# A planner that orders a four-layer transformer block: exclusive PSUM banks, gathered modulation matmuls, settled operands, sixteen passes

## The chip, the core and the metric

The kernel runs on one core of one Trainium2 chip. The time is device microseconds for one execution. Five instruction queues matter: TensorE (PE; its weight loads are PEld), VectorE (DVE), ScalarE (ACT), GpSimd (POOL) and SyncE (SP), which issues the transfers from HBM. TensorE writes its results into PSUM, eight banks of 512 float32 columns on 128 partitions. ScalarE and VectorE read them from there.

## What is computed

256 latent and 256 context tokens of width 1024 pass four layers. Layer i uses the token mixer i mod 3: grouped-query attention, neighbourhood attention with a bias, latent attention with compressed keys and values; so the fourth layer is the first kind again. Each is followed by a gated feed-forward part of width 2816, and around each part stands a modulation computed from the conditioning vector:

```python
mod = cond_lat @ w_ada[i] + b_ada[i]
sh1, sc1, g1, sh2, sc2, g2 = jnp.split(mod[:, None, :], 6, axis=-1)
h = modulate(x, sh1, sc1)                      # x * (1 + scale) + shift
y, yc = mixer(h, hc, ...)                      # kind = i % 3
x = layer_norm(DEEPNORM_ALPHA * x + g1 * y, ln_g[i, 0], ln_b[i, 0])
f = swiglu(modulate(x, sh2, sc2), w_ffn_gate[i], w_ffn_up[i], w_ffn_down[i])
x = layer_norm(DEEPNORM_ALPHA * x + g2 * f, ln_g[i, 1], ln_b[i, 1])
```

The context tokens take the same path with their own modulation in all layers but the last, where only the 256 latent tokens are left.

## The kernel before

Features lie on partitions, tokens on the free axis: eight tiles `x0` to `x7` of 128 x 512, latent tokens in the first 256 columns. Every float32 operand of a matrix product is split into a rounded high part (float32r) and a low part: ScalarE copies the high part out (`hh`, `whi`, `qh`, `gh`, `pth`), VectorE or GpSimd subtracts to get the low part (`hl`, `wlo`, `ql`, `gl`, `ptl`), and `mm3` forms three products, high by high, high by low, low by high. A product's sums stand in a `ps` tile, one PSUM bank; the tags `mm`, `sc`, `o` and `tp` have two banks each.

Weights come as `raw` tiles of 128 x 1024 (four buffers). Two tiles ahead of use `fetch` issues the transfer on SP, the copy on ScalarE and the subtraction on VectorE or GpSimd.

Three kinds of products stand on TensorE. "R" are float32r products. "T" are transposes through `ident`. "F" are plain float32 products, which write four blocks of 32 partitions: the first layer's modulation, in two parts (`ada_first`, 32 groups of four products `ps<-rawa,condp` with 128 columns; `ada_rest`, eight groups of four with 512 columns), and the sums of the norms (`Norm.sums`, sixteen products of 64 columns with `ones`, on `zs`, `x`, `sq`, `sq`). There are 14 such norm sums: two behind every attention and feed-forward part, one for each kind of token, and in the last layer one each, for which TensorE has nothing else to do. The modulation of the other layers is done on VectorE (`ada_vector`).

Attention works on 128 queries at a time: a score product into an `sc` bank, VectorE's negated maximum `nm`, ScalarE's exponent `p`, VectorE's reciprocal `r`, GpSimd's scaling of `p`, four transposes into a `tp` bank, the split into `pth`/`ptl` (or `ptch`/`ptcl`), and the value products. In the second layer, two heads of width 64 share a block of 128 features; `stacked` takes the queries or keys out of one bank by halves of 64 partitions. For keys that is, for each half: two ScalarE copies `stk` out of the bank and two VectorE subtractions `stl` that read the bank again:

```python
nc.scalar.activation(t[r], ps[r], AF.Copy)
nc.scalar.activation(t[o], ps[r], AF.Copy)
nc.vector.tensor_sub(t2[r], ps[r], f(t[r]))
nc.vector.tensor_sub(t2[o], ps[r], f(t[r]))
```

None of this is emitted where it is written. From a certain place on `nc` is the `Planner`: `note` records each operation with an estimated duration (`cost`), its operands and dependencies (`touch`; a PSUM tile counts as a whole), and `emit` makes the order. It runs `PASSES` rounds. In each, `backward` gives every operation a due time and a rank from the TensorE order of the round before, and `schedule` plays the list of operations: an engine that is free takes from its ready operations the one with the lowest due time (for TensorE, the lowest rank), with some rules that hold an engine back for an urgent operation about to become ready. The round with the shortest planned span wins, and its operations are emitted in the order of their planned starts. The names that the change touches there:

- `kind`: R, T or F. After a T the planner prefers another T whose rank lies within `STAY` of the best R; a turn to R from T or F costs `TURN`.
- `o.ready`: when the last dependency is done; `soon` and `ripe`: an engine's operations that become ready, and that are ready.
- `best`: the shortest span and its starts.
- `last`: when a buffer comes free. Two readers of one bank have no dependency in the planner. The tile framework beneath it, which sets the semaphores by the order in which operations are emitted, lets engines take turns on a bank.

## Time and profile before

| | us |
|---|---|
| median of three runs | 2086.41 (2084.97 to 2087.51) |
| the profiled execution, own time | 2086.06 |
| its span in the profile | 2083.9 |
| TensorE busy | 2040.6 (98%) |
| VectorE busy | 1481.7 (71%) |
| ScalarE busy | 961.9 (46%) |
| GpSimd busy | 402.5 (19%) |
| transfers, mean over the span | 144 GB/s |

The layers stand one behind the other. The start and the first attention take the first 208 us or so, the second layer's attention lies between 572 and 832 us, the third's between 1196 and 1404, the fourth's begins near 1768; the feed-forward parts lie between them. A matrix product's row in the timeline begins where it is issued and lasts beyond the start of the next one, since products are pipelined; the time that a product costs is read from one start to the next. Rows that follow each other with the same text are merged, and an F product has two rows in the trace.

### The profile page before, as it was taken

The page shows a single profiled execution, that of the slowest core. Times are in us where ns is not written, and L with a number is a line of the kernel's source. Part 1 is how long each engine was busy: PE and PEld are TensorE (multiplying, and loading weights), DVE is VectorE, ACT ScalarE, POOL GpSimd, SP SyncE. Part 2 cuts the span into 40 slices and gives each one's busy share as a digit, 9 for nine tenths or more (in the row PEclk, how much of TensorE's full clock was granted, in tenths as well). Part 3 has the DMA queues.
Part 4 walks back from the last instruction along what each step waited for, and adds up shares of the span by engine and source line. Part 5 has one row for each costly group of instructions (what it writes and reads, how often), then busy time and mean ns, then how long its engine had stood idle before and what let it go on. Part 6 is the DMA issues. An engine that isn't in the chain of part 4 may idle for free.

```text
span 2083.9 us, 31923 instructions
## 1 busy us (share of the span) xinstructions
PE 2040.6 (98%) x12048; PEld 1760.2 (84%) x12048; DVE 1481.7 (71%) x2549; ACT 961.9 (46%) x1686; POOL 402.5 (19%) x508
## 2 busy tenths in 40 slices
PE   8999999999999999999999999999999999989997
PEld 4788988888888888988888898898888888789997
DVE  4687988786487776888786376659777755975554
ACT  4574722223386665722223386745222234766443
POOL 0334300000342234300000343251000005441002
PEclk9999999999999999999999999999999999999999
DMA  9424466665222212466555231126555642334552
GB/s 369 160 82 142 160 194 212 195 219 173 87 87 82 81 62 82 143 197 202 172 197 162 64 94 55 42 75 200 186 188 177 199 143 72 99 122 142 185 189 72
DMA packets 92121, 300.17 MB, mean 144 GB/s; under 512 B 11328, under 2 KB 11456, under 8 KB 91968
## 3 DMA queue, kind: packets, MB, share of 16 engines
q1 hardware_dynamic: 91968, 298.14, 44.0%
q8 instruction: 95, 1.56, 0.3%
q14 instruction: 58, 0.48, 0.1%
HBM read 297.05 MB, written 1.05 MB: 143 GB/s over the span
## 4 chain that ended last, share of the span: by engine, by line
PE 91%; ACT 3%; DVE 3%; DMA 1%; issue 1%; SPq 0%; POOL 0%; DVEq 0%; ACTq 0%; POOLq 0%
PE ps L164 91%; ACT stk L164 1%; ACT p L164 1%; DMA rawa<-in_w_ada 1%; DVE stl L164 1%; ACT whi L164 1%; DVE nm L164 1%; DMA raw<-in_a_wo 0%; ACT pth L164 0%; DVE junk L164 0%; ACT x L164 0%; DVE wlo L164 0%; SPq L164 0%; DVE ptl L164 0%; DVE x L164 0%
## 5 line engine op out<-in xcount | busy, mean ns | idle before, releaser
L164 ACT ACTIVATE whi<-raw 128x1024 fp32r<-128x1024 f32 (+3 forms) x371 | 379.7, 1028 | 714.0 <-PE ps L164 421.7
L164 PE MATMUL ps<-hh,whi 128*128 128x512 f32 (+1 forms) x1648 | 582.0, 355 | 1.7 <-ACT hh L164 1.7
L164 PE MATMUL ps<-hh,wlo 128*128 128x512 f32 (+1 forms) x1648 | 581.2, 353 | 0.0
L164 PE MATMUL ps<-hl,whi 128*128 128x512 f32 (+1 forms) x1648 | 580.8, 353 | 0.0
L164 DVE TENSOR_TENSOR wlo<-raw,whi 128x1024 fp32r<-128x1024 f32 (+3 forms) x359 | 442.5, 1237 | 110.4 <-ACT whi L164 107.4
L164 DVE SCALAR_TENSOR_TENSOR junk<-raw,sil 128x1024 bf16<-128x1024 f32 x320 | 392.3, 1226 | 126.4 <-DMA raw<-in_w_ada 123.6
L164 PEld LDWEIGHTS ps<-hh,whi 128*128 128x128 f32 x1648 | 312.3, 190 | 42.8 <-ACT hh L164 1.9
L164 PEld LDWEIGHTS ps<-hh,wlo 128*128 128x128 f32 x1648 | 312.7, 190 | 42.0
L164 PEld LDWEIGHTS ps<-hl,whi 128*128 128x128 f32 x1648 | 312.8, 190 | 40.9
L164 PE MATMUL ps<-gh,whi 128*128 128x512 f32 (+1 forms) x800 | 271.9, 341 | 0.0
L164 PE MATMUL ps<-gh,wlo 128*128 128x512 f32 (+1 forms) x800 | 271.7, 341 | 0.0
L164 PE MATMUL ps<-gl,whi 128*128 128x512 f32 (+1 forms) x800 | 271.6, 340 | 0.0
L164 DVE SCALAR_TENSOR_TENSOR x<-ps,G,x 128x256 f32<-128x256 f32 x224 | 102.2, 480 | 131.8 <-PE ps L164 131.4
L164 POOL TENSOR_TENSOR zs<-x,x 128x256 f32<-128x256 f32 x14 | 12.2, 873 | 844.4 <-DVE x L164 844.4
L164 PEld LDWEIGHTS ps<-gh,whi 128*128 128x128 f32 x800 | 151.5, 190 | 17.3
L164 PEld LDWEIGHTS ps<-gh,wlo 128*128 128x128 f32 x800 | 151.4, 190 | 17.0
L164 PEld LDWEIGHTS ps<-gl,whi 128*128 128x128 f32 x800 | 151.5, 190 | 17.0
L164 POOL TENSOR_SCALAR p<-p,r 128x512 f32<-128x512 f32 (+1 forms) x144 | 91.3, 641 | 271.7 <-DVE r L164 253.4
L164 PE MATMUL ps<-whi,hh 128*128 128x512 f32 (+3 forms) x352 | 124.1, 353 | 1.1 <-DVE v L164 1.1
L164 PE MATMUL ps<-wlo,hh 128*128 128x512 f32 (+3 forms) x352 | 120.7, 344 | 0.0
L164 PE MATMUL ps<-whi,hl 128*128 128x512 f32 (+3 forms) x352 | 119.7, 344 | 0.0
L164 PE MATMUL ps<-oh,whi 128*128 128x256 f32 (+1 forms) x352 | 108.7, 315 | 0.5 <-ACT p L164 0.3
(205 smaller groups left out, 3102.9 us busy)
## 6 DMA issues: line engine op xcount, KB each, us to landing
raw<-in_w_gu SPq DMA_DIRECT2D x176, 512.0 KB, 4.2
raw<-in_w_ada SPq DMA_DIRECT2D x160, 512.0 KB, 4.0
raw<-in_w_d SPq DMA_DIRECT2D x64, 448.0 KB, 4.0
rawa<-in_w_ada SPq DMA_DIRECT2D x64, 256.0 KB, 5.6
raw<-in_w_d SPq DMA_DIRECT2D x32, 512.0 KB, 3.7
raw<-in_a_qkv SPq DMA_DIRECT2D x24, 512.0 KB, 4.1
raw<-in_a_wo SPq DMA_DIRECT2D x16, 512.0 KB, 3.5
raw<-in_b_qk SPq DMA_DIRECT2D x16, 512.0 KB, 3.3
```

Of the source, the lines that this page charges most:

```text
L164: op.fn = lambda: getattr(getattr(self.nc, queue), method)(*p, **k)
```

## The change

It changes the planner, and no operation, tile or size. Six things are new:

- ScalarE and VectorE exclude each other on a PSUM tile. `op.banks` lists the PSUM tiles that an operation of these two engines touches, and `held` keeps until when the last of them, and on which engine, has such a tile. An operation that comes too early goes back to `soon`. An operation with a bank is also not taken to fill a gap.
- F products are gathered: having issued an F, the planner prefers another F within `STAY`, as it did for T; and a turn into F costs `TURN` as well.
- Settled operands: for TensorE, an operation whose last dependency on another engine (`fresh`) is less than `CALM` = 0.3 us old gives way to the best one whose operands are older.
- Sixteen rounds for eight.
- Two costs: a float32 product of 65 to 128 columns 0.06 for 0.085 us, transfers 357 for 370 GB/s.
- The winning round's starts and ends are written back before emitting.

```diff
-    PASSES = 8
+    PASSES = 16
+    CALM = 0.3
@@ cost
-            return 0.083 if n <= 64 else 0.085 if n <= 128 else 0.242
+            return 0.083 if n <= 64 else 0.06 if n <= 128 else 0.242
...
-            return n * out.shape[0] * 4 / 370e3
+            return n * out.shape[0] * 4 / 357e3
@@ touch
+            if ap.space == bass.MemoryType.PSUM and op.eng in ("ACT", "DVE"):
+                op.banks.append(t.name)
@@ schedule
-        def release(o, t):
+        def release(o, t, own=False):
             o.ready = max(o.ready, t)
+            if not own:
+                o.fresh = max(o.fresh, t)
...
             o = ops[e["ripe"][0][1]]
+            free = max([held[n][0] for n in o.banks if n in held and held[n][1] != o.eng], default=0.0)
+            if free > t:
+                heapq.heappop(e["ripe"])
+                heapq.heappush(e["soon"], (free, o.idx))
+                continue
...
-                    fit = [x for x in e["ripe"] if ops[x[1]].dur <= r - t + self.SLIP]
+                    fit = [x for x in e["ripe"] if ops[x[1]].dur <= r - t + self.SLIP and not ops[x[1]].banks]
...
-            if o.eng == "PE" and kind == "T" and o.kind == "R":
-                more = [x for x in e["ripe"] if ops[x[1]].kind == "T" and x[0] < o.rank + self.STAY]
+            if o.eng == "PE" and o.fresh > t - self.CALM:
+                calm = [x for x in e["ripe"] if ops[x[1]].fresh <= t - self.CALM]
+                if calm:
+                    x = min(calm)
+                    e["ripe"].remove(x)
+                    e["ripe"].append((o.rank, o.idx))
+                    heapq.heapify(e["ripe"])
+                    o = ops[x[1]]
+            if o.eng == "PE" and kind in ("T", "F") and o.kind != kind:
+                more = [x for x in e["ripe"] if ops[x[1]].kind == kind and x[0] < o.rank + self.STAY]
...
-                if o.kind == "R" and kind != "R":
+                if o.kind != kind and (kind != "R" or o.kind == "F"):
                     o.end += self.TURN
...
+            for n in o.banks:
+                held[n] = o.end + self.FROM[o.eng], o.eng
```

What this does to the order shows in three places. The first is TensorE at the third layer's start, where the norm sum `ps_2292` (latent tokens, from the second layer's feed-forward part) stands among the first products of the new layer (`whi_2238` and the like). Before:

```order
L164 MATMUL ps_2287<-whi_2238,hh1_2250 128x320
L164 MATMUL ps_2292<-zs_2214,ones_83 32x64 x2
L164 MATMUL ps_2287<-wlo_2239,hh1_2250 128x320
L164 MATMUL ps_2292<-zs_2214,ones_83 32x64 x2
L164 MATMUL ps_2287<-whi_2238,hl1_2258 128x320
L164 MATMUL ps_2292<-x7_107,ones_83 32x64 x2
L164 MATMUL ps_2288<-whi_2238,hh0_2249 128x320
L164 MATMUL ps_2292<-x7_107,ones_83 32x64
L164 MATMUL ps_2288<-wlo_2239,hh0_2249 128x320
L164 MATMUL ps_2292<-x7_107,ones_83 32x64
L164 MATMUL ps_2292<-sq_2213,ones_83 32x64
L164 MATMUL ps_2288<-whi_2238,hl0_2257 128x320
```

With the change:

```order
L165 MATMUL ps_2287<-whi_2238,hh1_2250 128x320
L165 MATMUL ps_2292<-zs_2214,ones_83 32x64 x4
L165 MATMUL ps_2287<-wlo_2239,hh1_2250 128x320
L165 MATMUL ps_2287<-whi_2238,hl1_2258 128x320
L165 MATMUL ps_2292<-x7_107,ones_83 32x64 x4
L165 MATMUL ps_2292<-sq_2213,ones_83 32x64 x4
L165 MATMUL ps_2292<-sq_2281,ones_83 32x64 x4
L165 MATMUL ps_2288<-whi_2238,hh0_2249 128x320
L165 MATMUL ps_2288<-wlo_2239,hh0_2249 128x320
```

The sixteen F products stood in nine runs (the rest of the last four follows below the rows shown) and stand in two now. Over the whole program the F runs go from 63 to 35.

The second is TensorE in the second layer, behind the last product of the key block `ps_1309` (products on `ps_1320` belong to the next query or key block, `ps_1328` is a transpose of probabilities, `ps_1321` are the scores that use the new keys, `ps_1298` a value product, `ps_1331` a later score). Before:

```order
L164 MATMUL ps_1309<-hh7_1112,wlo_1245 128x512
L164 MATMUL ps_1320<-hh0_1105,whi_1294 128x512
L164 MATMUL ps_1320<-hl0_1113,whi_1294 128x512
L164 MATMUL ps_1320<-hh0_1105,wlo_1295 128x512
L164 MATMUL ps_1320<-hh1_1106,whi_1294 128x512
L164 MATMUL ps_1320<-hl1_1114,whi_1294 128x512
L164 MATMUL ps_1320<-hh1_1106,wlo_1295 128x512
L164 MATMUL ps_1328<-ident_78,p_1289 128x128 x4
L164 MATMUL ps_1321<-stk_1313,stk_1304 128x256
L164 MATMUL ps_1320<-hh2_1107,whi_1294 128x512
L164 MATMUL ps_1320<-hl2_1115,whi_1294 128x512
L164 MATMUL ps_1321<-stl_1314,stk_1304 128x256
```

With the change, the last twelve rows up to the first use of `stl_1314`:

```order
L165 MATMUL ps_1298<-pth_1282,v_1181 128x256
L165 MATMUL ps_1298<-ptl_1283,v_1181 128x256
L165 MATMUL ps_1298<-pth_1282,v_1182 128x256
L165 MATMUL ps_1298<-ptl_1283,v_1182 128x256
L165 MATMUL ps_1298<-pth_1282,v_1171 128x256
L165 MATMUL ps_1298<-ptl_1283,v_1171 128x256
L165 MATMUL ps_1298<-pth_1282,v_1172 128x256
L165 MATMUL ps_1298<-ptl_1283,v_1172 128x256
L165 MATMUL ps_1331<-stk_1313,stk_1304 128x512
L165 MATMUL ps_1320<-hh3_1108,whi_1294 128x512
L165 MATMUL ps_1320<-hl3_1116,whi_1294 128x512
L165 MATMUL ps_1321<-stl_1314,stk_1304 128x256
```

Ahead of these stand, as before, the six products on `ps_1320`, the transposes and the first product on `stk_1313`, and then three products on `ps_1320`. So eight narrow and four wide products more stand before the first product that reads `stl_1314`.

The third is ScalarE at the same block; behind a row stand the semaphores that it waits for (each engine has its own). Before:

```order
L164 ACTIVATE p_1301,su_1302<-ps_1299,nm_1300 128x512 [waits DVE_49,PE_49]
L164 ACTIVATE ptch_1310<-ps_1312 128x512 [waits PE_49]
L164 ACTIVATE stk_1313<-ps_1309 64x512 [waits PE_49]
L164 ACTIVATE stk_1313<-ps_1309 64x512
L164 ACTIVATE stk_1315<-ps_1309 64x512 [waits DMAHW0_49,DVE_49]
L164 ACTIVATE stk_1315<-ps_1309 64x512 [waits DVE_49]
L164 ACTIVATE pth_1326<-ps_1328 128x512 [waits PE_49]
L164 ACTIVATE whi_1355<-raw_1354 128x1024 [waits DMAHW2_49]
```

With the change:

```order
L165 ACTIVATE p_1301,su_1302<-ps_1299,nm_1300 128x512 [waits DVE_49,PE_49]
L165 ACTIVATE ptch_1310<-ps_1312 128x512 [waits PE_49]
L165 ACTIVATE stk_1313<-ps_1309 64x512 [waits PE_49]
L165 ACTIVATE stk_1313<-ps_1309 64x512
L165 ACTIVATE stk_1315<-ps_1309 64x512 [waits Activation_49]
L165 ACTIVATE stk_1315<-ps_1309 64x512
L165 ACTIVATE pth_1326<-ps_1328 128x512 [waits PE_49]
L165 ACTIVATE whi_1355<-raw_1354 128x1024 [waits DMAHW3_49]
```

The same eight instructions; those on `stk_1315` no longer wait for VectorE. On VectorE the four `stl` of this block follow each other now, and the maximum of the next scores, which stood ahead of the last one, follows behind it.

## Rows read from the trace of the kernel before

**Rows 1.** Busy time in us of each engine over the span, from the table by stage.
```profile
sum 2083.90, PE 2040.59 PEld 1760.19 DVE 1481.70 ACT 961.94 POOL 402.52; mean PE 156.97 PEld 135.40 DVE 113.98 ACT 74.00 POOL 30.96
```

**Rows 2.** The same table by stage: from:to, length; PE, PEld, DVE, ACT, POOL busy; clock, DMA.
```profile
...
18.00:52.00 34.00, 33.98 (x232) 20.88 (x233) 17.11 (x41) 16.36 (x27) 0.00 (x0) 1.00 1.05 390
52.00:208.00 156.00, 152.23 (x933) 122.27 (x932) 122.89 (x240) 91.00 (x182) 59.31 (x85) 1.00 0.37 128
...
260.00:520.00 260.00, 260.00 (x1149) 215.29 (x1148) 208.10 (x327) 69.18 (x84) 0.00 (x0) 1.00 0.63 199
...
572.00:832.00 260.00, 251.13 (x1657) 221.70 (x1657) 193.55 (x348) 173.82 (x358) 93.13 (x112) 1.00 0.24 79
...
1768.00:1924.00 156.00, 145.47 (x1000) 133.39 (x1000) 119.76 (x221) 104.77 (x201) 49.90 (x69) 0.96 0.37 116
...
```

**Rows 3.** Waits of TensorE, 572 to 832 us: total us, times, longest.
```profile
PE ps L164 <- DVE stl L164: 4.8, 6, 1.1
PE ps L164 <- ACT p L164: 1.3, 3, 0.7
PE ps L164 <- DVE v L164: 1.1, 3, 0.5
...
```

**Rows 4.** Timeline, TensorE, norm sum at the third layer's start: start, length, instruction.
```profile
...
1205.91 0.31 PE L164 MATMUL ps<-whi,hh 128*128 128x320 f32 x1
1206.14 0.30 PE L164 MATMUL ps<-zs,ones 128*32 128x64 f32 x4
1206.38 0.41 PE L164 MATMUL ps<-wlo,hh 128*128 128x320 f32 x1
1206.72 0.31 PE L164 MATMUL ps<-zs,ones 128*32 128x64 f32 x4
...
```

**Rows 5.** Timeline, TensorE, last norm sum of the first layer's feed-forward part, context tokens.
```profile
...
566.10 0.28 PE L164 MATMUL ps<-gh,whi 128*128 128x256 f32 x1
566.22 0.28 PE L164 MATMUL ps<-gl,whi 128*128 128x256 f32 x1
...
566.66 0.39 PE L164 MATMUL ps<-gh,wlo 128*128 128x256 f32 x1
...
567.55 0.39 PE L164 MATMUL ps<-gh,whi 128*128 128x256 f32 x1
567.77 0.28 PE L164 MATMUL ps<-gl,whi 128*128 128x256 f32 x1
...
```

**Rows 6.** Timeline, TensorE, a modulation product of 512 columns (one F run).
```profile
...
59.90 1.04 PE L164 MATMUL ps<-rawa,condp 128*32 128x512 f32 x2
60.88 0.50 PE L164 MATMUL ps<-whi,hh 128*128 128x512 f32 x1
...
```

**Rows 7.** Timeline, all engines, a key block of the second layer; [idle before <- releaser].
```profile
651.37 0.39 PE L164 MATMUL ps<-hh,wlo 128*128 128x512 f32 x1
...
651.80 1.20 ACT L164 ACTIVATE stk<-ps 64x512 fp32r<-64x512 f32 x2 [1.47 <-PE ps L164]
...
653.03 0.68 DVE L164 TENSOR_TENSOR stl<-ps,stk 64x512 fp32r<-64x512 f32 x1 [1.97 <-ACT stk L164]
...
653.74 0.59 ACT L164 ACTIVATE stk<-ps 64x512 fp32r<-64x512 f32 x1 [0.75 <-DVE stl L164]
...
654.37 0.68 DVE L164 TENSOR_TENSOR stl<-ps,stk 64x512 fp32r<-64x512 f32 x1 [0.66 <-ACT stk L164]
...
655.11 0.39 PE L164 MATMUL ps<-stl,stk 128*128 128x256 f32 x1 [0.96 <-DVE stl L164]
...
```

**Rows 8.** Timeline, TensorE, the next key block of the second layer.
```profile
671.50 0.39 PE L164 MATMUL ps<-hh,wlo 128*128 128x512 f32 x1
...
675.10 0.38 PE L164 MATMUL ps<-stl,stk 128*128 128x256 f32 x1 [0.74 <-DVE stl L164]
...
```

**Rows 9.** Timeline, TensorE, last layer, scores of its second head.
```profile
...
1811.67 0.79 PE L164 MATMUL ps<-kh,qh 128*128 128x512 f32 x1 [2.56 <-ACT p L164]
1812.27 0.63 PE L164 MATMUL ps<-kl,qh 128*128 128x512 f32 x1
...
```

More of the change, by code (lines that the diff above doesn't have):

```diff
@@ L48 @@
     __slots__ = ("eng", "fn", "dur", "deps", "users", "tiles", "idx", "table", "left", "ready", "due", "start", "end",
-                 "kind", "port", "rank", "pace")
+                 "kind", "port", "rank", "pace", "banks", "fresh")
 class Planner:
@@ L165, in note @@
         op.deps, op.users, op.tiles = set(), [], []
+        op.banks = []
         for ap, w in [(x, False) for x in ins] + [(x, True) for x in outs]:
@@ L212, in emit @@
             if best is None or span < best[0]:
-                best = span, [o.start for o in self.ops]
+                best = span, [(o.start, o.end) for o in self.ops]
             aim = [o.start if o.eng == "PE" else g for o, g in zip(self.ops, goal)]
         self.span, start = best
-        for o in sorted(self.ops, key=lambda o: (start[o.idx], o.idx)):
+        for o in self.ops:
+            o.start, o.end = start[o.idx]
+        for o in sorted(self.ops, key=lambda o: (o.start, o.idx)):
             o.fn()
@@ L248, in schedule @@
             o.left = len(o.deps) + sum(slot[t] is None for t in o.tiles)
-            o.ready = 0.0
+            o.ready = o.fresh = 0.0
             for t in o.tiles:
@@ L269, in schedule @@
         kind = "R"
+        held = {}
         while done < len(ops):
@@ L326, in schedule @@
             for u in o.users:
-                release(u, o.end + self.hop(o, u))
+                release(u, o.end + self.hop(o, u), u.eng == o.eng)
             for n in o.tiles:
```

## Prediction

> **What bounds the kernel now.** I read the busy times of the whole span first [rows 1]: TensorE is busy 2040.6 of 2083.9 us, its weight loads, which lie under its products, 1760.2, and the next engine, VectorE, 1481.7. So the time is TensorE's list of products plus the places where it stands still or turns, and the other engines matter only where TensorE waits for them. The table by stage [rows 2] says where that is. In the first feed-forward stretch (260 to 520 us) it runs 1149 products in 260.00 us without a gap, 0.226 us each; nothing can be saved there except products. In the first layer's attention it lacks 3.8 of 156 us, in the second layer's 8.9 of 260, at the last layer's attention 10.5 of 156. The waits of the second layer [rows 3] name VectorE's `stl` (4.8 us), ScalarE's `p` (1.3) and VectorE's `v` (1.1). What the busy share hides is what TensorE loses while it counts as busy: the plain-float32 products (modulation from `condp`, norm sums from `ones`; "F" below, the others "R") come in small runs, and each run costs a turn into it and out of it [rows 4, 5]. The change alters no product and no tile; it alters order alone. In the feed-forward stretches where TensorE is full its order is the same word for word, and SP's transfers hardly move (15 of 635 change place, by two at most). So the sum has terms at the start, in the attention stages and at their borders only.
>
> **F runs.** The price of a run comes from the norm sum at the third layer's start, where two products on `zs` alternate with one R product: from one run to the next 0.58 us [rows 4], of which the R product (320 columns, 320/512 of 0.226) is 0.14. So a short run costs about 0.44. The common form is one F product, one R product, then fifteen F: from 566.22 to 567.77 it is 1.55 us with three R products of 0.12, so 1.19 for two runs [rows 5]; the sixteen in one run are then 1.19 less one short run, about 0.77. I take 0.42 for a run that disappears, between 0.40 and 0.44.
> Norm sums: leaving out the last two, which end in waits, the order before has 31 runs for twelve sums, the changed one 14. Seventeen fewer at 0.42 are 7.1 us. Nothing hides them: TensorE is the full engine around these sums (no idle time stands in rows 4 and 5).
> Modulation of the first layer's first part: after the opening run the order before has 19 runs, the changed one 9. Ten at 0.42 are 4.2 us, if TensorE and not the transfers sets the pace; from 18 to 52 us it is busy 33.98 of 34.00 [rows 2], so it does. But the vectors that follow the last run (`hh6`) come no sooner after it, and eleven R products stand between the two before, seven now: four at 0.226, 0.9 us, may be waited for. I take the whole loss: 3.3. The ends are 4.2 and zero.
> Modulation's second part (512 columns): ten runs become nine, and a run with one product takes 0.98 until the next R product starts [rows 6]: 1.0 us.
> Together 11.4 us.
>
> **The excluded bank.** Take the 16 split halves of the second layer's keys (`stk` by ScalarE, then `stl` by VectorE, each reading 64 partitions of one bank). At 653 us the engines take strict turns [rows 7]: VectorE 653.03 to 653.71, ScalarE from 653.74, VectorE again from 654.37. ScalarE's halves have no use for what VectorE writes there; it waits for the bank. The planner before lets them overlap, so it puts the first product on `stl` too early: TensorE stands 0.96 us before 655.11. From the bank's last product (651.37) to that one are 3.74 us, 1.13 of them lost and 2.61 of work (a wait costs some 0.17 more than its idle time, since a product's row lasts 0.39 where the next could start after 0.226).
> The change puts the four ScalarE halves in a row, then VectorE's. That delays `stl`: 0.43 until ScalarE starts, 4 x 0.60, 0.03, 2 x 0.68, 0.06 to TensorE are 4.3 us [rows 7]. And it puts eight 256-column and four 512-column products more ahead of the consumer: 2.61 + 0.96 + 0.90 = 4.47. So the wait is gone with 0.17 to spare; three places have this form: 3.4 us. Two have that of 671.50 to 675.10 [rows 8], with 0.74 idle and so 0.9 lost; the work in between grows by six 256-column products and a transpose, 0.8. Some of that may find the halves not yet there; I take 0.7 each, 1.4. The sixth wait I leave. The three waits for `v` (1.1 us idle, 1.6 lost [rows 3]) get four transposes and a 256-column product ahead of them, 0.5 us: 1.5 us. Sum 6.3.
> What is late next: the score product of that head's context part now has 13 instead of 17 512-column products and 5 instead of 13 256-column ones before its transposes, 1.9 us less, and VectorE's maximum stands behind all four `stl` instead of between the last two. How much room that chain had no row tells; it gets later by one `stl`, 0.68 at most, so between nothing and 0.7 us may be waited for at each of three heads: 0.3 each, 0.9 back. Net 5.4, with ends 7.5 and 0.
>
> *A page's rule beside it.* In rows 7 ScalarE and VectorE are never inside the bank together, though the `stk` of 653.74 reads other partitions than the `stl` before it. The Trainium skill, "PSUM — Partial Sum Buffer", section "PSUM bank collisions raise a hardware error", says two engines collide only in the same bank and the same 32 partitions, and that different quadrants may be read at once. By that rule the exclusion is stricter than the chip needs, the planner before would have had the better picture, and this term would be nothing; by the rows the semaphores of both programs take turns bank by bank, and the term stands. I keep the rows; the other outcome is priced as the first rival.
>
> **Settled operands, transfers, passes.** These show in the order only as moved products. In the first layer's attention the last heads gain distance (the transposes of one head stand behind 24 narrow products instead of 7), others lose it (one of the second group had 24 narrow products, 12 transposes and 6 wide products between scores and transposes, and has 6, 8 and 6). Idle there is 3.8 us [rows 2]; I take 0, with ends 3 gained and 3 lost. At the last layer TensorE already waits 2.56 us for ScalarE's probabilities and then runs slower for a while (0.60 from that start to the next [rows 9], where 0.226 is usual). The changed order comes to that wait three 512-column products sooner: 0.7 us lost. The third layer has no wait worth naming: 0, half a microsecond either way.
>
> **Sum.** -11.4 - 5.4 + 0.7 = -16.1 us. The profiled execution took 2086.06, so 2069.9; the median of the runs is 0.35 above it: 2070.3 us.
>
> **Rivals.**
> *Given back at the chain.* The bank's exclusion is met, but the second layer is held by the chain scores, maximum, exponent, scaling, transposes, so TensorE reaches the next wait sooner by what it saved. Then only the runs and the last layer count: -11.4 + 0.7, and 2075.7 us. For it: VectorE is busy 194 and ScalarE 174 of 260 us there, and heads alternate closely. Against: of the named waits that chain (`p`) has 1.3 us, `stl` and `v` have 5.9 [rows 3]. The page's rule above would end at the same time: with nothing to exclude there is nothing to win.
> *Slower.* Nearness to scores. Counting by the durations above the blocks of scores whose transposes now stand less than 5.2 us of work behind them, and nearer than before, I find 15 in four layers. If each waits 1.7 us on average (two thirds of the 2.56 of rows 9, with the slow restart behind it), that costs 25 us against the 16.8 gained and more than undoes the runs: 2086.4 - 16.8 + 25 = 2094.6. It decides from about 1.1 us each. Against: over the second layer's heads, some of them as near to their scores already, `p` costs 1.3 us in all [rows 3], and the same order gives other heads more room.
> *It does not do what it says.* The turn is paid inside the following product, or the order of issue does not set the time, and the runs are worth nothing: 2086. Against it stand the 0.58 us of rows 4, which repeat through a whole sum.
>
> **How the numbers follow.** The forecast (2063 to 2074) has 0.70, the give-back (around 2076) 0.18, no effect 0.05, slower 0.07. Low end: 12.5 from the runs, 7.5 from the bank, 3 from the first attention give 2063.4. At the top the give-back with zero gain at the start is 2079, and a little of the slower case lies below 2081. Range 2063 to 2081. A measurement of this kernel tells about 0.2%, 4.2 us, from no change: faster means below 2082.2. Faster 0.87, same 0.06, slower 0.07.
>
> **What would show it.** Right: sixteen `ones` products in one run with R products only around them; no `stl` wait near the 653 form, ScalarE's four halves end to end; the TensorE gap of the second layer down from 8.9 to about 3 us; the feed-forward stretches unchanged. Wrong: `p` as the new name in the second layer's waits, a wait on `hh6` at the end of the start longer than 0.9 us, or several waits of 1 to 2 us before transposes in the first attention. A longer wait at the last layer's scores, with a longer slow stretch behind it, would eat a few of the 16.

## The result, and the profile after

The median of four runs is 2066.27 us (2065.74 to 2067.43); four runs of the kernel before beside it have 2086.76. The ratio is 0.9904, 95% interval 0.9887 to 0.9921, so 20.5 us less where 16.1 were forecast; 2066.3 lies in the range of 2063 to 2081. The profiled execution took 2066.53 us, 19.5 less than that of before, with a span of 2064.7, 19.2 less.

The table by stage of the changed kernel (columns as in [rows 2], whose rows it answers; the last line answers [rows 1]; stages behind the first move forward by a few us):

```profile
...
18.00:52.00 34.00, 34.00 (x252) 24.46 (x252) 19.82 (x50) 19.67 (x35) 0.00 (x0) 1.00 1.04 386
...
260.00:520.00 260.00, 260.00 (x1148) 215.36 (x1148) 204.96 (x321) 68.32 (x84) 0.00 (x0) 1.00 0.63 196
...
572.00:832.00 260.00, 256.71 (x1725) 228.58 (x1727) 195.44 (x361) 176.88 (x364) 100.26 (x116) 0.99 0.24 80
...
1768.00:1924.00 156.00, 145.85 (x1080) 137.46 (x1079) 115.52 (x203) 96.50 (x181) 45.55 (x60) 0.96 0.40 128
...
sum 2064.00, PE 2027.80 PEld 1758.37 DVE 1477.53 ACT 955.85 POOL 416.44; mean PE 168.98 PEld 146.53 DVE 123.13 ACT 79.65 POOL 34.70
```

From 18 to 52 us TensorE has 252 rows of products instead of 232, without a gap: the same time, more work in it. The feed-forward stretch from 260 to 520 us is as it was. In the second layer TensorE lacks 3.3 of 260 us where it lacked 8.9. TensorE's busy time falls by 12.8 us though it has the same products: that part was lost while busy.

A norm sum (timeline, TensorE, the first layer's feed-forward part; answers [rows 5]):

```profile
560.93 0.28 PE L165 MATMUL ps<-gl,whi 128*128 128x256 f32 x1
561.14 0.32 PE L165 MATMUL ps<-zs,ones 128*32 128x64 f32 x8
561.28 0.29 PE L165 MATMUL ps<-x,ones 128*32 128x64 f32 x8
561.39 0.41 PE L165 MATMUL ps<-sq,ones 128*32 128x64 f32 x16
561.72 0.39 PE L165 MATMUL ps<-gh,wlo 128*128 128x256 f32 x1
```

All sixteen F products (32 rows) stand in one run, 0.79 us from the R product before to the one behind, of which 0.12 is the R product: 0.67 for the run, where the two runs of [rows 5] cost 1.19.

A key block of the second layer (timeline, TensorE, ScalarE, VectorE; answers [rows 7]):

```profile
643.55 0.39 PE L165 MATMUL ps<-hh,wlo 128*128 128x512 f32 x1
...
643.98 2.41 ACT L165 ACTIVATE stk<-ps 64x512 fp32r<-64x512 f32 x4 [1.47 <-PE ps L165]
...
646.42 2.81 DVE L165 TENSOR_TENSOR stl<-ps,stk 64x512 fp32r<-64x512 f32 x4 [3.19 <-ACT stk L165]
...
647.82 0.39 PE L165 MATMUL ps<-hl,whi 128*128 128x512 f32 x1
...
648.05 0.28 PE L165 MATMUL ps<-stl,stk 128*128 128x256 f32 x1
```

ScalarE's four halves stand end to end and VectorE's four behind them. From the block's last product to the first product on `stl` are 4.50 us and no wait; the first two halves are done at 647.82 (half of the 2.81 behind 646.42), 0.23 ahead of that product. Less the 0.06 that TensorE took from the last half to the product in [rows 7], 0.17 are to spare. Forecast were 4.47 of work and 0.17 to spare.

The waits of TensorE from 572 to 832 us (total, times, longest; answers [rows 3]):

```profile
PE ps L165 <- DVE ptcl L165: 1.5, 1, 1.5
PE ps L165 <- DVE stl L165: 0.9, 2, 0.4
PE ps L165 <- ACT p L165: 0.5, 2, 0.3
PE ps L165 <- POOL hl L165: 0.3, 1, 0.3
```

`stl` falls from 4.8 to 0.9, and the two that are left are those of the form of [rows 8]. A new name heads the list, `ptcl`. Its place (timeline, TensorE, the last heads of the second layer):

```profile
778.65 0.40 PE L165 MATMUL ps<-stl,stk 128*128 128x512 f32 x1
780.54 0.81 PE L165 MATMUL ps<-ident,p 128*128 128x128 f32 x4 [1.49 <-DVE ptcl L165]
781.15 0.79 PE L165 MATMUL ps<-oh,whi 128*128 128x512 f32 x1
781.74 0.63 PE L165 MATMUL ps<-ol,whi 128*128 128x512 f32 x1
782.17 0.63 PE L165 MATMUL ps<-oh,wlo 128*128 128x512 f32 x1
```

Behind the wait the products of 512 columns stand 0.43 us apart where 0.226 is usual, for some four microseconds: the granted clock from 780 to 790 us is 0.83 of 2.4 GHz in the mean, and 0.43 us is the pitch at the lower of its two levels, 1.2 GHz.

### The profile page after: what moved, and what is told of

Same layout as the page of the kernel before. It is cut to its first block, busy times and chain, and to the rows that moved or that the text cites. A ratio compares the mean times of both kernels' runs of the same rounds, so it can differ in the third digit from the quotient of the medians.

```text
span 2064.7 us, 31918 instructions
## 1 busy us (share of the span) xinstructions
PE 2027.8 (98%) x12048; PEld 1758.4 (85%) x12048; DVE 1477.5 (72%) x2549; ACT 955.9 (46%) x1684; POOL 416.4 (20%) x508
## 4 chain that ended last, share of the span: by engine, by line
PE 91%; DVE 4%; ACT 2%; issue 1%; DMA 1%; POOL 0%; SPq 0%; DVEq 0%; ACTq 0%; POOLq 0%
PE ps L165 91%; DVE wlo L165 1%; DVE nm L165 1%; ACT stk L165 1%; DVE stl L165 1%; DVE x L165 0%; ACT p L165 0%; DVE ptl L165 0%; ACT whi L165 0%; DMA bada<-in_b_ada 0%; DMA rawa<-in_w_ada 0%; DVE ps L165 0%; DVE stk L165 0%; POOL sq L165 0%; ACT x L165 0%
## 5 line engine op out<-in xcount | busy, mean ns | idle before, releaser
L165 POOL TENSOR_SCALAR p<-p,r 128x512 f32<-128x512 f32 (+1 forms) x144 | 98.9, 693 | 253.2 <-DVE r L165 232.7
L165 PE MATMUL ps<-oh,wlo 128*128 128x256 f32 (+1 forms) x352 | 109.3, 316 | 0.0
```

The lines of the kernel that those rows point to most:

```text
L165: op.fn = lambda: getattr(getattr(self.nc, queue), method)(*p, **k)
```

## Where the time went, stage by stage

Only by stages can the experiments be compared. A mark is a TensorE product before which two programs have issued the same set of products; the table gives by how much the stretch between two marks became longer or shorter against the kernel before (us, one profiled execution each; the marks are times of before). The second layer is cut at 780 us, where its last heads and its output product begin. The last column ends at the last TensorE product.

| | to 54 | 54-572 | 572-780 | 780-832 | 832-1404 | 1404-1768 | 1768-end | all |
|---|---|---|---|---|---|---|---|---|
| changed kernel | -4.5 | -1.1 | -7.4 | 1.2 | -5.1 | -0.8 | -1.6 | -19.2 |
| runs alone | -5.8 | 0.2 | 0.4 | -0.3 | -3.3 | -0.8 | -3.6 | -13.3 |
| exclusion alone | -0.6 | -0.2 | -5.9 | -1.0 | 0.0 | 0.0 | -2.3 | -9.9 |
| settled operands alone | -2.9 | 3.5 | -0.7 | 1.3 | -1.4 | 0.0 | -3.2 | -3.4 |
| passes and costs alone | -1.8 | -1.8 | -0.1 | -0.2 | 0.2 | 0.0 | -2.7 | -6.4 |
| without the exclusion | -5.5 | -2.1 | -0.9 | 0.0 | -4.3 | -0.8 | -1.1 | -14.7 |
| without the runs | -1.6 | -1.2 | -7.3 | 0.4 | -2.4 | 0.2 | -1.4 | -13.2 |
| without settled operands | -5.3 | -1.8 | -5.0 | 2.5 | -4.7 | -0.8 | -1.3 | -16.4 |
| sums split into pairs | -5.2 | 4.4 | -4.7 | 2.5 | 5.8 | 4.5 | -1.5 | 5.9 |
| other last layer | -4.8 | -1.1 | -7.3 | 1.0 | -5.1 | -0.8 | -2.7 | -20.8 |
| and other 780-832 | -4.2 | -1.1 | -7.4 | 0.2 | -5.1 | -0.7 | -3.6 | -22.0 |
| second layer: TensorE changed | -4.4 | -0.5 | -0.4 | 15.5 | -4.5 | -0.8 | -1.4 | 3.4 |
| second layer: the others changed | -4.8 | -1.1 | 2.8 | 9.9 | -4.5 | -0.7 | -1.4 | 0.1 |

## Experiments: each part alone

Four kernels add one part each to the planner of before, three take one part out of the changed one. All ratios are against runs of the kernel before, taken beside them on the same chip, with 95% intervals.

**The runs alone**: eight rounds, old costs, no exclusion, `CALM = 0`.

```diff
-            if o.eng == "PE" and kind == "T" and o.kind == "R":
+            if o.eng == "PE" and kind in ("T", "F") and o.kind != kind:
...
-                if o.kind == "R" and kind != "R":
+                if o.kind != kind and (kind != "R" or o.kind == "F"):
```

> The kernel before with the gathering of F products alone (preference for another F, and the turn into F priced); eight rounds, old costs, no exclusion, no settled operands. Its order has 37 F runs where before has 63. Theory (each part pays for itself): 26 runs fewer at 0.42 us are 10.9 us, less up to 0.9 at the start: 10 us faster, about 2076.7. The stl waits of the second layer stay (about 0.96 us three times, 0.74 twice). Rival (the gain is the plan as a whole, found by more rounds): within 4 us of before.

Measured: 2074.04 us, ratio 0.9937 [0.9925, 0.9950], 37 runs of F products for 63. 12.9 us less, of which 5.8 lie at the start, 3.3 in the stage of the third layer (2.8 at its norm sum of [rows 4]), and 3.6 in the last layer, in which no run changed. Without that last part the table has 9.7, where 10 were expected.

**The exclusion alone**, eight rounds, old costs, old rule for F, `CALM = 0`:

```diff
+            free = max([held[n][0] for n in o.banks if n in held and held[n][1] != o.eng], default=0.0)
+            if free > t:
+                heapq.heappop(e["ripe"])
+                heapq.heappush(e["soon"], (free, o.idx))
+                continue
...
-                    fit = [x for x in e["ripe"] if ops[x[1]].dur <= r - t + self.SLIP]
+                    fit = [x for x in e["ripe"] if ops[x[1]].dur <= r - t + self.SLIP and not ops[x[1]].banks]
...
+            for n in o.banks:
+                held[n] = o.end + self.FROM[o.eng], o.eng
```

> The kernel before with the exclusion of ScalarE and VectorE on a bank alone. 61 F runs (before 63). The work between a key block's last product and the first product on stl is 4.0 us at the three places that had 2.6, and 3.0 at the two that had 2.55; 4.3 and about 3.5 would cover it. Theory: the three waits fall from 0.96 to about 0.1 to 0.3 us, the two from 0.74 to about 0.3, sum some 3.5 us, and 0.8 for two runs: about 2082.5. Rival (the bank rule adds nothing, the chain of scores takes back what is saved): 2086, with p as the name of the new waits.

Measured: 2076.84 us, 0.9949 [0.9937, 0.9962]. The second layer gets 6.9 us shorter, more than the 4.3 expected for the whole run. Waits of TensorE from 552 to 835 us:

```profile
PE ps L165 <- ACT p L165: 1.3, 1, 1.3
PE ps L165 <- ACT stk L165: 0.4, 1, 0.4
PE ps L165 <- DVE stl L165: 0.4, 2, 0.2
...
```

**Settled operands alone:**

```diff
+    CALM = 0.3
...
+            if o.eng == "PE" and o.fresh > t - self.CALM:
+                calm = [x for x in e["ripe"] if ops[x[1]].fresh <= t - self.CALM]
...
```

> The kernel before with the preference for settled operands alone. 58 F runs, 2.95 and 2.78 us of work ahead of stl. Theory: five runs fewer are 2.1 us, the stl waits shrink by 0.35 three times and 0.23 twice, 1.5 us: about 2083. Rival (this is the part that carries the change, by removing small waits everywhere): 10 us faster or more, 2077 or less.

Measured: 2083.83 us, 0.9984 [0.9975, 0.9992]. The stages go both ways, +3.5 in the first attention, -3.2 in the last layer. The time lies near the 2083 expected, but not by the places that were named: `stl` still costs 4.2 us of waiting in the second layer. It looks more like another draw of the search than like a gain with a place; no run shows which.

**Sixteen rounds and the two costs alone:**

```diff
-    PASSES = 8
+    PASSES = 16
...
-            return 0.083 if n <= 64 else 0.085 if n <= 128 else 0.242
+            return 0.083 if n <= 64 else 0.06 if n <= 128 else 0.242
...
-            return n * out.shape[0] * 4 / 370e3
+            return n * out.shape[0] * 4 / 357e3
```

> The kernel before with sixteen rounds and the two new costs alone. 58 F runs, stl as before (2.60 and 2.55 us of work ahead of it). Theory: five runs fewer, 2.1 us, all else unchanged: about 2084.5. Rival (more rounds find the better plan): 2076 or less.

Measured: 2080.32 us, 0.9967 [0.9955, 0.9979]. Again the last layer (-2.7) holds the largest part.

The four parts alone add up to 12.9 + 10.1 + 3.1 + 6.6 = 32.7 us, the whole change brings 20.5. The table says why in part: the four have 11.1 us together at the start, where the whole has 4.5, and each of them has 2.3 to 3.6 us in the last layer, 11.8 together, where the whole has 1.6. Of those 11.8, 3.7 (0.8 to 1.1 each) stand behind the last layer's wait for `hh`, where TensorE stays at the lower clock for 3.4 to 3.9 us in these four and for 5.8 before; the last layer's experiment below shows that this differs between kernels of one order too.

**Without the exclusion**, all else as changed:

```diff
-            if free > t:
-                heapq.heappop(e["ripe"])
-                heapq.heappush(e["soon"], (free, o.idx))
-                continue
...
-                    fit = [x for x in e["ripe"] if ops[x[1]].dur <= r - t + self.SLIP and not ops[x[1]].banks]
+                    fit = [x for x in e["ripe"] if ops[x[1]].dur <= r - t + self.SLIP]
...
-            for n in o.banks:
-                held[n] = o.end + self.FROM[o.eng], o.eng
```

> The changed kernel without the exclusion on a bank. 36 F runs (changed kernel 35), 2.95 and 2.78 us of work ahead of stl. Theory: the stl waits come back to about 0.6 us three times and 0.5 twice, the v waits in part: 4 us slower than the changed kernel, about 2070.5. Rival (exclusion not needed): 2066.

Measured: 2071.07 us, 0.9929 [0.9912, 0.9946]. The second layer's gain falls from 6.2 to 0.9 us, and `stl` is back in TensorE's waits (552 to 835 us):

```profile
PE ps L165 <- DVE stl L165: 4.2, 6, 1.0
PE ps L165 <- ACT p L165: 1.8, 4, 0.6
...
```

So this term belongs to the exclusion, shown by adding it and by taking it out.

**Without the runs:**

```diff
-            if o.eng == "PE" and kind in ("T", "F") and o.kind != kind:
+            if o.eng == "PE" and kind == "T" and o.kind == "R":
...
-                if o.kind != kind and (kind != "R" or o.kind == "F"):
+                if o.kind == "R" and kind != "R":
```

> The changed kernel without the gathering of F products. 55 F runs (changed kernel 35), stl distances as in the changed kernel. Theory: 20 more runs at 0.42 us are 8.4 us: about 2074.7, with no new wait in the second layer. Rival: 2066 to 2069.

Measured: 2073.32 us, 0.9939 [0.9924, 0.9954], with 55 runs of F products for 35: 7.0 us for 20 runs, 0.35 each (6.0 and 0.30 by the two profiled executions).

**Without settled operands:**

```diff
-    CALM = 0.3
+    CALM = 0.0
```

> The changed kernel without the preference for settled operands. 33 F runs, 4.0 and 3.2 us of work ahead of stl. Theory: two runs fewer win 0.8 us, the stl waits come back by some 0.3 us at five places: about 2067. Rival (settled operands carry small waits in all attention stages): 2072 or more.

Measured: 2069.09 us, 0.9915 [0.9900, 0.9930]. 2.8 us are gone: 3.7 in the second layer, with some won in the first attention; the interval overlaps that of the changed kernel, so this is not resolved.

## Experiment: the price of a run

The changed order as it is, but ten norm sums cut into eight pairs, with the seven R products that stood ahead of the sum put between them. No operation is added.

```diff
-        for o in sorted(self.ops, key=lambda o: (o.start, o.idx)):
+        line = sorted(self.ops, key=lambda o: (o.start, o.idx))
+        for o in self.apart(line):
             o.fn()
...
```

> The order of the changed kernel, all engines, with one difference: at ten norm sums the seven R products that stood ahead of the sixteen F products are put between them, one behind every two. 105 F runs for 35, no other product moved. Theory (a run has a price of its own): 70 more runs at 0.42 us are 29.4 us: about 2095.7, and 0.58 us from run to run as in the kernel before. Rival (the turn is hidden or paid once for a sum): within 4 us of 2066.

Measured: 2092.04 us, 1.0028 [1.0018, 1.0038]: slower than before the change. 70 more runs cost 25.8 us, 0.37 each. Timeline, TensorE, inside such a sum:

```profile
564.25 0.39 PE L165 MATMUL ps<-gl,whi 128*128 128x256 f32 x1
564.57 0.31 PE L165 MATMUL ps<-sq,ones 128*32 128x64 f32 x4
564.81 0.39 PE L165 MATMUL ps<-gh,wlo 128*128 128x256 f32 x1
565.12 0.31 PE L165 MATMUL ps<-sq,ones 128*32 128x64 f32 x4
565.36 0.39 PE L165 MATMUL ps<-gh,whi 128*128 128x256 f32 x1
```

0.55 from pair to pair, 0.12 of it the R product: 0.43 for a pair. TensorE waits for nothing in these rows, and still loses the time while it counts as busy. The rival that the order of issue doesn't set the price is out.

## Experiment: the last layer

TensorE in the changed kernel at the last layer's scores (answers [rows 9]):

```profile
1791.80 0.38 PE L165 MATMUL ps<-ident,qn 128*128 128x128 f32 x2
1794.80 0.80 PE L165 MATMUL ps<-kh,qh 128*128 128x512 f32 x1 [2.62 <-ACT p L165]
1795.39 0.63 PE L165 MATMUL ps<-kl,qh 128*128 128x512 f32 x1
1795.82 0.63 PE L165 MATMUL ps<-kh,ql 128*128 128x512 f32 x1
```

The wait is that of before, and so is the stretch at 0.43 behind it. The order of the runs alone has no such wait there (1.3 at the longest). The next kernel takes the changed order up to the last layer's attention, and the order of the runs alone from there:

```diff
+        first = self.order_of("after")
+        second = self.order_of("runs")
+        line = self.splice(first, second, TAIL)
...
+    def splice(self, one, two, cut):
+        head = one[:next(i for i, o in enumerate(one) if o.idx == cut)]
+        seen = set(head)
+        return head + [o for o in two if o not in seen]
```

> The changed order up to the last layer's attention (1768 us), and from there the order of the kernel with the runs alone. Nothing is left out. Theory: the changed order loses its gain in the last layer because TensorE waits 2.6 us for ScalarE's p there and then runs a stretch at the lower clock; the order of the runs alone has no wait above 1.3 us there and gained 3.7 us from 1768 to the end, where the changed one gained 1.6. So 2.1 us less than the changed kernel: 2064.2 us, and a granted clock of 1.00 from 1790 to 1820. Rival: the clock falls at this place whatever is waited for, because of what the layers before did; then the time stays at 2066.3 and the clock at 0.94.

Measured: 2065.23 us (2061.28 to 2065.59), 0.9893 [0.9879, 0.9906]. The granted clock from 1790 to 1800 us is 1.00, in the changed kernel it is 0.83 (table by stage, the changed kernel, then this one):

```profile
1790.00:1800.00 10.00, 6.70 (x26) 5.03 (x27) 7.64 (x19) 6.69 (x16) 5.00 (x10) 0.83 0.00 2
```

```profile
1790.00:1800.00 10.00, 8.21 (x48) 6.13 (x47) 9.22 (x23) 9.24 (x21) 6.76 (x12) 1.00 0.06 25
```

At the mark of 1820 us the kernel is 4.8 us ahead of where it began the layer, the changed one 0.4; of these 4.8, 2.1 are lost again by 1871 us, 1.3 of them in a wait for `qh` that ends at 1799.27, behind which the clock stays. So the wait and the slow stretch are the cause of what the changed kernel lacks there (of 4.4 us, 2.6 are the wait and some 1.5, an estimate from the two pitches, the products behind it), and half of it is given back at once. The net, 1.1 us by the table and 1.0 by the medians, is smaller than the 2.1 expected and not resolved by the intervals.

What the two orders do differently ahead of the wait shows on ScalarE. Between a square root (`sd`) and an exponent (`p`) it has a row `ACT_TABLE_LOAD` of 1.28 us (timeline, ScalarE, the changed kernel, then this one):

```profile
1792.67 1.28 ACT L165 ACT_TABLE_LOAD   x1
1793.97 0.69 ACT L165 ACTIVATE p<-ps,nm 128x512 f32<-128x512 f32 x1
```

```profile
1788.40 1.28 ACT L168 ACT_TABLE_LOAD   x1
1790.34 0.69 ACT L168 ACTIVATE p<-ps,nm 128x512 f32<-128x512 f32 x1 [0.66 <-DVE nm L168]
```

In the changed kernel `p` follows the load at once, so 1.28 of the 2.62 us are that load, and it is the same before (1809.55 to 1810.83). In the other order the load is over 0.66 us before the maximum `nm` is there. No run moved the load alone.

Behind 1871 us the last layer's column holds something that is not order. Every kernel waits there for `hh` (1.67 us, 1.88 without settled operands), and behind it TensorE's products stand at the lower clock's pitch for a time that differs between kernels with the same products in the same order. Timeline, TensorE, the changed kernel and one that has its order from the last attention on (TensorE's order alone, below); the second row of each is the first at the usual pitch:

```profile
1858.38 1.65 PE L165 MATMUL ps<-hh,whi 128*128 128x256 f32 x6 [1.67 <-ACT hh L165]
...
1862.92 0.29 PE L165 MATMUL ps<-hh,whi 128*128 128x256 f32 x1
```

```profile
1880.39 1.65 PE L168 MATMUL ps<-hh,whi 128*128 128x256 f32 x6 [1.67 <-ACT hh L168]
...
1886.61 0.29 PE L168 MATMUL ps<-hh,wlo 128*128 128x256 f32 x1
```

That is 4.5 and 6.2 us; the kernel before has 5.8. Against it the column gains 0.5 by this in the changed kernel, 0.1 in the kernel of this section, and 0.9 in the runs alone, which has the same products as the kernel of this section from the last attention on. So a difference of up to one microsecond in that column says nothing of an order.

**And the end of the second layer**, 780 to 832 us, in the order of the exclusion alone, spliced in the same way:

> As the run before, and the end of the second layer (780 to 832 us) in the order of the kernel with the excluded bank alone. Theory: the changed order loses 1.2 us there to a new wait (ptcl before transposes), the other order gains 1.0 there, so another 2.2 us less: 2062.0. Rival: the wait belongs to the chain of the last head and comes with any order that reaches it sooner; then the 1.2 us stay and the time is that of the run before.

Measured: 2064.20 us (2063.48 to 2064.59), 0.9891 [0.9876, 0.9906]. The wait for `ptcl` and the lower clock behind it are gone, a wait of 1.3 us for `p` stands there instead, and the stretch costs 0.2 instead of 1.2: 1.0 us of the 2.2 expected. By its median this is the fastest order seen (the single fastest execution, 2061.28, is one of the kernel above). Its runs all lie below those of the changed kernel (2065.74 at least), which were not taken beside them, and the ratios' intervals overlap: the gain is not resolved.

## Experiment: whose order is it

The exclusion moves two things: ScalarE's and VectorE's instructions on the bank, and how much TensorE does before it reads `stl`. I held the second for what counts. Two kernels cross the orders of before and after in the second layer, engine by engine; everything outside it is the changed order.

```diff
+        line = {e: [o for o in (new if (e == "PE") == AFTER_ON_PE else old) if o.eng == e] for e in self.ENGINES}
```

> In the second layer (567 to 832 us) TensorE keeps the changed order, and ScalarE, VectorE, GpSimd and the transfers go back to the order of before (but for a few instructions at the end that would not fit); the rest is the changed kernel. Theory (distance): what the exclusion gains is that the planner knows how late stl will be and puts more products ahead of its first reader (4.47 us for 2.60); the turns of the two engines on the bank as before make stl ready 3.74 us after the last product, so it is in time, and the layer keeps its gain: 2066 to 2068 us, stl waits under 1.5 us. Rival (row order): the gain comes from ScalarE's halves end to end and VectorE's behind them; then most of the 6.1 us of the layer go, 2070 to 2073.

Measured: 2088.86 us, 1.0008 [1.0000, 1.0017].

> The reverse: in the second layer TensorE has the order of before, ScalarE, VectorE, GpSimd and the transfers the changed one; the rest is the changed kernel. Theory (distance): stl is ready 4.3 us after the block's last product, TensorE comes to it after 2.6, so it waits 1.7 us at three places and about 1 at two more; the layer is no better than before and rather 1 to 2 us worse: 2072.5 to 2075, stl waits of 5 to 7 us. Rival (row order): 2066 to 2069.

Measured: 2085.92 us, 0.9998 [0.9989, 1.0007].

Both lose the whole gain of the change, 22.6 and 19.7 us. Most of it goes from 780 to 832 us (15.5 and 9.9), where the last heads meet the output product and a few instructions had to change places; from that stretch I read the waits and the clock, and nothing for or against either theory. Over the heads in the middle (624 to 730 us) TensorE of the changed kernel waits for `stl` alone, 0.9 us. With TensorE's order alone, and then with the other engines' order alone, its waits there are:

```profile
PE ps L168 <- DVE v L168: 1.4, 2, 0.7
PE ps L168 <- DVE stl L168: 1.1, 2, 0.6
PE ps L168 <- POOL p L168: 0.7, 2, 0.4
```

```profile
PE ps L168 <- DVE stl L168: 3.8, 4, 1.6
PE ps L168 <- DVE v L168: 1.0, 3, 0.3
```

The step on distance holds as far as it goes: with TensorE's order alone `stl` is waited for 1.1 us, with the other engines' order alone it gets worse, 1.6 at the longest, where 4.3 - 2.6 = 1.7 was worked out. But the distance alone isn't the gain. From 624 to 728 us TensorE's order alone has 2.4 of the changed kernel's 4.6 us, the others' alone loses 0.5; over the whole layer to 780 us they are -0.4 and +2.8 against -7.4 together. Where TensorE comes later to `stl`, VectorE's old order gives it `v` too late. My theory, that TensorE's distance is nearly all of it, fell; its rival, that the rows on the bank alone do it, fell too. The two orders go together. What these kernels cross is every order of the other engines, transfers included; one that exchanges the rows on the bank alone was not tried.

## Why the prediction came out as it did

The profiled execution is 19.5 us faster and the medians 20.5, where 16.1 were forecast. Of the 3.3 us that the table below has more than the forecast, 2.3 lie in the last layer, 1.2 in the first part of the modulation and 0.7 in the third layer; the modulation's second part gives 0.8 less, and the rest agrees to 0.1. Two slips in the sums change nothing: 2086.06 less 16.1 is 2070.0, and the runs' terms at their best, 7.1, 4.2 and 1.0, are 12.3 for the 12.5 of the low end.

The price of all F runs can be read from the traces directly: from the start of the R product ahead of a run to that of the R product behind it, less the usual 0.227, 0.147 or 0.120 us of that product. The other terms are the stages of the table above without the runs in them; the measured column adds up to -19.4, the table to -19.2.

| term | forecast | measured |
|---|---|---|
| norm sums, 17 fewer runs | -7.1 | -7.1 (15.8 to 8.7) |
| first part of the modulation | -4.2, +0.9 given back | -3.9 (10.0 to 6.0); nothing given back, and 0.6 more besides |
| second part | -1.0 | -0.2 |
| second layer | -6.3, +0.9 given back | -7.0 to 780 us, +1.6 behind it: -5.4 |
| first attention | 0, 3 either way | +0.1 |
| third layer | 0, 0.5 either way | -0.7 |
| last layer | +0.7 | -1.6 |

**The runs** are right in step and size. By these rows 27 runs fewer save 11.0 us, 0.41 each; the two experiments give 0.35 and 0.37 as means over larger changes.

**The second part of the modulation** lost its gain: one run less saved 1.1, but behind another (90.14 us, ahead of a score product) TensorE waits for `p` (0.45 idle), and up to the next product it takes 0.95 us longer than such a run elsewhere. The term was made by counting runs alone, without reading what stands behind each.

**The wait on `hh6`** that was to give back 0.9 at the start did not come; no wait stands there. It was a guess at a chain whose room no row told, taken at its full size.

**The second layer** comes out at the forecast -5.4, but by two errors that cancel. The heads gained 7.0 where 6.3 were counted, since the first head's waits, which the sum left at nothing, went too (from 567 to 624 us 1.6 us in four places before, 0.3 now). The give-back is 1.6 for 0.9 and stands elsewhere: not at the maximum of three heads but once, at the end, at `ptcl` with the slow stretch behind it. The rival "given back at the chain" had the right mechanism there, at a third of its size.

**The last layer** is the step that failed: 0.7 lost was forecast from three products fewer ahead of the wait for `p`, and 1.6 were gained. The same products stand ahead of that wait in both orders, and the three only come earlier, ahead of the transposes on `qn`. A loss is there all the same: by the mark of 1815 us the changed kernel has lost 0.9 since 1768, 0.65 of it ahead of the wait, where it now waits 0.4 for `qh`; the wait for `p` is 2.62 for 2.56. The term ended its count there. Behind it 1.3 are won by 1820, where a second wait for `p` (0.73 before) is gone; 0.65 more by 1849, where neither kernel has a wait to speak of; and 0.55 behind the wait for `hh`, with the shorter stretch at the lower clock. The kernels above show how loosely this stretch hangs on the change: every one of the four single parts gains 2.3 to 3.6 us there.

**Nearness to scores**, the slower rival, needed 1.1 us at each of 15 places; `p` costs 0.5 us in the second layer, nothing in the third, and 1.1 in the first attention (0.5 at the longest), where it cost 2.5 before.

**The page's rule.** By the Trainium skill, "PSUM — Partial Sum Buffer", section "PSUM bank collisions raise a hardware error", reads of different quadrants of 32 partitions of a bank do not collide, so halves of 64 partitions need not exclude each other. By that rule the exclusion would have been worth nothing. The run with the exclusion alone gains 6.9 us in the second layer and 10.1 in all. In the rows the engines take turns on a bank in both programs, so this is no evidence against the rule on the chip: the semaphores that the framework sets are wider than it. Whether halves that overlap would be better still wasn't tried, since those semaphores are not the kernel's to leave out.

What stays open: how much of what settled operands, passes and costs bring is theirs and how much is another draw of the search. Their single kernels move stages that they have no reason to move, by 3 us up and down.

## What to carry to other kernels

Count the runs of plain float32 products, not the products: here a run between float32r products cost 0.35 to 0.42 us on a full TensorE, which no wait and no idle time shows. Where a planner doesn't know a resource that the engines exclude each other on, teach it the resource and plan everything anew; half of the new order, put into the old, gave back all it had gained (most of it where the halves met at the layer's end). And look behind each long wait of TensorE for products twice as far apart: the wait is then only part of the price.

## What the runs showed of the hardware that I had not expected

A wait of 1.5 us at 780 us was followed by a granted clock of 0.83 over the next 10 us, products 0.43 instead of 0.227 apart, as was one of 2.6 at the last layer; a wait of 1.3 us (in the kernel with both splices, and at `qh` in the last layer) and one of 1.6 (at the last layer without settled operands) left it at 1.00. So the wait's length alone does not tell which it is. At the start the column of the granted clock is no guide: behind waits of 2.8 us (before) and 1.8 us (changed) the 512-column products stand 0.43 us apart until 22.2 and 22.8 us, and the column reads 1.00 from 18 to 52 us, as the trace's clock record begins at 22.5 and 23.1. The pitch of the products is the surer sign. In the kernel with TensorE's order alone, where waits of up to 3.3 us follow each other at the second layer's end, the clock was 0.50 for ten microseconds on end (table by stage):

```profile
790.00:800.00 10.00, 4.49 (x19) 3.27 (x18) 5.56 (x10) 3.32 (x6) 1.75 (x3) 0.71 0.17 54
800.00:810.00 10.00, 6.74 (x27) 5.96 (x27) 3.86 (x6) 4.98 (x9) 0.69 (x1) 0.50 0.06 13
```

The stretch became 15.5 us longer. 11.1 of that are TensorE's idle time there (12.65 for 1.55 us); that the products at the lower clock are most of the other 4.4 is an estimate from this difference.
